# Two decoder layers on one core: pre-norm vectors multiplied onto the transposed activations, a fixed order for the first steps, and memory tokens turned by VectorE and DMA

## The chip, the cores and the metric

The kernel runs on one core of a Trainium2 chip. The metric is device microseconds from launch to end, the median of several runs. Five engines work side by side: TensorE (PE; its weight loads are listed apart as PEld), VectorE (DVE), ScalarE (ACT), GpSimd (POOL) and SyncE (SP). Each runs its own instructions in the order of its queue, and they meet at semaphores. In this kernel SP and POOL issue nearly all DMAs.

## The reference: what is computed

Two layers over 256 tokens of width 1024, all in float32. Each layer has three sub-layers, and each of these normalises its input with a vector of weights (the pre-norm), works, and normalises again before adding to the stream:

```python
def rms_norm(x, g):
    y = x * lax.rsqrt(jnp.mean(x * x, axis=-1, keepdims=True) + EPS)
    return y * g
def swiglu(h, w_in, w_out):
    a, b = jnp.split(h @ w_in, 2, axis=-1)
    return (jax.nn.silu(a) * b) @ w_out
for l in range(2):
    h = rms_norm(x, ffn1_norm_pre[l])
    x = x + 0.5 * rms_norm(swiglu(h, ffn1_w_in[l], ffn1_w_out[l]), ffn1_norm_post[l])
    h = rms_norm(x, mix_norm_pre[l])
    y = token_mixer(h, mem, ..., mem_norm[l], ...)   # conv, sparse attention, 256 memory tokens
    x = x + rms_norm(y, mix_norm_post[l])
    h = rms_norm(x, ffn2_norm_pre[l])
    x = x + 0.5 * rms_norm(swiglu(h, ffn2_w_in[l], ffn2_w_out[l]), ffn2_norm_post[l])
```

In the mixer the memory tokens are normalised with `mem_norm` and projected by `w_mem_kv` to keys and values. `w_in` of a feed-forward part is 1024 x 5632, `w_out` 2816 x 1024. Since a row's scale (the inverse root) factors out of a product, the kernel multiplies it on after the product; only the vector `g` has to meet the data or the weights before.

## The kernel before

**Products.** Every float32 operand is split into a high part (rounded to the format in which TensorE multiplies, fp32r) and a low part (the rest). A product of 128x128 by 128x512 is then three matmuls into one bank of PSUM: high by high, high activations by low weights, low activations by high weights (`mm3`, L337 to L340). Weights come from memory in units of 128x1024: SP loads `raw` (4 buffers), `split_unit` (L265) makes `whi` on ACT and `wlo` on DVE (8 buffers, four units). In units that follow a pre-norm the vector of that norm is multiplied on during this split, one value per row of weights, held in `gT` with one column per 128 rows (L280 and L281); where a unit holds two groups of 128 rows, each half of 512 columns is an instruction of its own. Other units are split plainly (L276 and L277).

**Activations.** `prenorm` (L442) turns x, 128 tokens by 1024, into 8 blocks of 128x128 with the tokens last: 8 transposes on PE into two banks (L381), then ACT rounds `hThi` out of PSUM (L372) and DVE subtracts `hTlo` (L373). The row scales (`rstd` L423, `rs` L450 to L453) run on ACT, DVE and POOL beside that. The mixer does the same with the merged branches before its output product.

**Turns.** The gated activations of a feed-forward part (`wide`, L501, made of two PSUM banks) go another way (`turn`, L388): DVE transposes blocks of 32x32 (`blocks`, L391), POOL writes them out in four DMAs (`there`, L396) and reads them back transposed in one (`moved`, L403); then ACT and DVE split them (`turnhi` L416, `turnlo` L417). A turn's parts are put into the program AWAY = 1, BACK = 3 and SPLIT = 8 steps after the transposition. The attention's probabilities take the same way.

**Memory.** `memory` (L605), one run per layer in the background, loads two tiles `m` of 128 memory tokens, calls `prenorm` on each (8 transposes on PE each), and then multiplies by `w_mem_kv`. `setup` (L534, called when the first output product of layer 1 has done 4 of 22 units) builds masks and loads small constants into `stage` by ten POOL DMAs (L587 to L591), which PE transposes (L593).

**Order.** Two streams, one per 128 tokens, are run as generators; a counter `now` of steps interleaves them, stream 0 ahead by up to LEAD = 3 steps. Both use the same weight unit, so a unit is 12 matmuls of 512 columns in the feed-forward input. Splits are put AHEAD = 4 steps before their use, loads 7. `later` defers a piece by some steps. A scheduler then orders every engine's instructions by its own model, except SP's queue, which stands in program order. PSUM has 6 banks for products and 2 for transposes.

**Start.** `keep_clock` (L164) runs 11 matmuls on a tile of zeros; the first vector is transposed on PE (L184) and copied to `gT` (L185); then x is transposed.

## Time and profile before

| what | value |
|---|---|
| median of 3 runs | 1281.77 us (1279.89 to 1281.87) |
| the profiled execution, its own time | 1282.43 us |
| its span, first to last instruction | 1280.5 us |
| mean granted TensorE clock | 0.996 of full speed |
| PE busy | 1259.4 us (98%) |
| DVE, ACT, POOL busy | 900.4, 770.7, 182.1 us |
| DMA | 280.58 MB, mean 219 GB/s |

The profile is of one execution. Its span begins with the first instruction and ends with the last; 1.93 us of its own time lie around that. The median of the runs is 0.66 us below the profiled execution. The busy times are read against the span: 98% of it on TensorE leaves 21.1 us in which it stood.

### The profile page before, as it was taken

The numbers are of one execution on the slowest core, as the hardware profiler recorded it, in microseconds if no ns is written. First come the engines' busy times: TensorE is split into PE (matmuls) and PEld (weight loads), VectorE is DVE, ScalarE is ACT, GpSimd is POOL, SyncE is SP. The second block draws the span as 40 slices with busy tenths as digits, with TensorE's granted clock in tenths as the row PEclk, the third lists the DMA queues.
The fourth block names the chain that finished last, engine by engine and source line by source line (L and its number), as shares of the span: only waits on it lengthen the run. The fifth ranks groups of instructions, "written<-read, shape, count | busy, mean of one in ns | idle before, by whom it ended". The sixth has DMA issues, their size and how long they took to land.

```text
span 1280.5 us, 16988 instructions
## 1 busy us (share of the span) xinstructions
PE 1259.4 (98%) x5898; PEld 1043.1 (81%) x5898; DVE 900.4 (70%) x1244; ACT 770.7 (60%) x1263; POOL 182.1 (14%) x384
## 2 busy tenths in 40 slices
PE   9999999999999999999999899999999999999996
PEld 7888788888888888888888788888888887888885
DVE  6767476879978676666566575668898876767752
ACT  6655366888875564554555455569887755555541
POOL 3101401302110011011001012013022100110110
PEclk9999999999999999999999999999999999999998
DMA  8777575776876657777767676757678756577770
GB/s 265 246 245 259 187 251 169 232 227 194 269 241 196 203 180 205 244 242 236 241 188 228 202 251 230 239 165 247 177 246 252 227 174 225 176 235 231 237 271 34
DMA packets 131877, 280.58 MB, mean 219 GB/s; under 512 B 11376, under 2 KB 30480, under 8 KB 131792
## 3 DMA queue, kind: packets, MB, share of 16 engines
q1 hardware_dynamic: 118256, 239.30, 59.6%
q0 software_dynamic: 13504, 40.20, 9.7%
q8 instruction: 46, 0.75, 0.2%
q14 instruction: 39, 0.32, 0.1%
q10 hardware_dynamic: 32, 0.01, 0.0%
HBM read 258.49 MB, written 20.97 MB: 218 GB/s over the span
## 4 chain that ended last, share of the span: by engine, by line
PE 89%; DMA 3%; ACT 2%; DVE 2%; issue 1%; POOL 1%; DVEq 0%; POOLq 0%; ACTq 0%
PE acc L338 19%; PE acc L340 19%; PE acc L339 19%; PE y L340 7%; PE y L339 6%; PE y L338 6%; PE pt L381 2%; DMA there<-blocks 2%; PE br L338 2%; PE br L340 2%; PE br L339 2%; PE o L856 1%; DMA moved<-there 1%; ACT whi L280 1%; PE s L834 1%
## 5 line engine op out<-in xcount | busy, mean ns | idle before, releaser
L280 ACT ACTIVATE whi<-raw,gT 128x512 fp32r<-128x512 f32 (+2 forms) x432 | 363.1, 873 | 232.2 <-PE acc L340 158.5
L281 DVE SCALAR_TENSOR_TENSOR wlo<-raw,gT,whi 128x512 fp32r<-128x512 f32 (+2 forms) x432 | 395.2, 936 | 153.1 <-ACT whi L280 151.2
L338 PE MATMUL acc<-whi,hThi 128*128 128x512 f32 (+1 forms) x1184 | 462.7, 391 | 4.1 <-DVE wide L501 3.2
L339 PE MATMUL acc<-wlo,hThi 128*128 128x512 f32 (+1 forms) x1184 | 459.6, 389 | 0.1
L340 PE MATMUL acc<-whi,hTlo 128*128 128x512 f32 (+1 forms) x1184 | 458.7, 388 | 0.0
L338 PEld LDWEIGHTS acc<-whi,hThi 128*128 128x128 f32 x1184 | 222.9, 188 | 48.1 <-DVE wide L501 3.6
L340 PEld LDWEIGHTS acc<-whi,hTlo 128*128 128x128 f32 x1184 | 222.7, 188 | 45.8 <-DVE hTlo L373 0.5
L339 PEld LDWEIGHTS acc<-wlo,hThi 128*128 128x128 f32 x1184 | 222.8, 188 | 43.4 <-DVE wlo L281 0.8
L277 DVE TENSOR_TENSOR wlo<-raw,whi 128x1024 fp32r<-128x1024 f32 x144 | 174.7, 1222 | 64.9 <-ACT whi L276 63.0
L276 ACT CAST whi<-raw 128x1024 fp32r<-128x1024 f32 x144 | 149.6, 1050 | 91.5 <-PE acc L340 50.9
L396 POOL DMA_DIRECT2D there<-blocks x160 | 87.9, 556 | 475.3 <-DVE blocks L391 472.0
L340 PE MATMUL y<-whi,turnlo 128*128 128x512 f32 x352 | 137.5, 391 | 0.0
L339 PE MATMUL y<-wlo,turnhi 128*128 128x512 f32 x352 | 137.4, 390 | 0.0
L338 PE MATMUL y<-whi,turnhi 128*128 128x512 f32 x352 | 136.4, 390 | 0.0
L417 DVE TENSOR_TENSOR turnlo<-moved,turnhi 128x1024 fp32r<-128x1024 f32 (+1 forms) x40 | 46.8, 1169 | 69.7 <-ACT turnhi L416 69.5
L416 ACT CAST turnhi<-moved 128x1024 fp32r<-128x1024 f32 (+1 forms) x40 | 40.3, 1008 | 79.4 <-DMA moved<-there 62.9
L339 PEld LDWEIGHTS y<-wlo,turnhi 128*128 128x128 f32 x352 | 66.1, 188 | 13.5
L340 PEld LDWEIGHTS y<-whi,turnlo 128*128 128x128 f32 x352 | 66.1, 188 | 13.5
L338 PEld LDWEIGHTS y<-whi,turnhi 128*128 128x128 f32 x352 | 66.0, 188 | 13.5
L431 POOL TENSOR_TENSOR nr<-nv,mhalf 128x1 f32<-128x1 f32 x28 | 19.0, 679 | 363.4 <-DVE nv L429 359.5
L403 POOL DMA_DIRECT2D moved<-there x40 | 22.4, 561 | 188.4 <-DMA there<-blocks 131.9
L496 ACT ACTIVATE th<-acc,rs 128x512 f32<-128x512 f32 (+1 forms) x48 | 30.9, 644 | 16.9 <-PE acc L340 16.9
(284 smaller groups left out, 1196.9 us busy)
## 6 DMA issues: line engine op xcount, KB each, us to landing
raw<-in_ffn_w_in_dram SPq DMA_DIRECT2D x160, 512.0 KB, 4.8
raw<-in_w_mix_in_dram SPq DMA_DIRECT2D x96, 512.0 KB, 4.7
raw<-in_ffn_w_out_dram SPq DMA_DIRECT2D x88, 512.0 KB, 5.0
there<-blocks POOLq DMA_DIRECT2D x128, 128.0 KB, 4.3
moved<-there POOLq DMA_DIRECT2D x32, 512.0 KB, 5.5
raw<-in_ffn_w_in_dram SPq DMA_DIRECT2D x32, 256.0 KB, 4.1
raw<-in_w_mem_kv_dram SPq DMA_DIRECT2D x16, 512.0 KB, 4.9
raw<-in_w_mix_out_dram SPq DMA_DIRECT2D x16, 512.0 KB, 4.3
```

The lines of the kernel that those rows point to most:

```text
L276: nc.scalar.copy(h, v)
L277: nc.vector.tensor_sub(w, v, f32(h))
L280: nc.scalar.activation(h, v, AF.Copy, scale=g)
L281: nc.vector.scalar_tensor_tensor(w, v, g, f32(h), op0=OP.mult, op1=OP.subtract)
L338: nc.tensor.matmul(ps, lhsT=xh, rhs=wh, start=start, stop=False, skip_group_check=skip)
L339: nc.tensor.matmul(ps, lhsT=xh, rhs=wl, start=False, stop=False, skip_group_check=skip)
L340: nc.tensor.matmul(ps, lhsT=xl, rhs=wh, start=False, stop=stop, skip_group_check=skip)
L381: nc.tensor.transpose(pt[:, j * P:(j + 1) * P], src[:, c0 + j * P:c0 + (j + 1) * P], ident)
L396: nc.gpsimd.dma_start(there[:, q * f:(q + 1) * f].rearrange("(p j) f -> j p f", j=32), blocks[q * 32:(q + 1) * 32, :n].rearrange("j (p f) ...
L416: nc.scalar.copy(hv, mv)
L417: nc.vector.tensor_sub(lv, mv, f32(hv))
L496: nc.scalar.activation(th[:, :n], pa[:, :n], AF.Tanh, scale=r_half)
```

## The change

1. The pre-norm vectors no longer go onto the weights. All units are split plainly, one instruction of 1024 columns per engine. `prenorm` multiplies the vector onto the transposed x: DVE writes `hf` from PSUM (two instructions of 128x512), ACT rounds `hThi` from `hf` in SBUF, DVE subtracts `hTlo`. In `product` the matmuls are ordered high by high for both banks, low activations for both, low weights for both.
2. In the first EARLY = 6 steps all instructions marked `pinned` keep program order. The start's 11 idle matmuls become 7 + 2 + 2 with the transposes between; splits are made 1 step ahead and the lead is 2 up to step RAMP = 10; the row scales come SCALES = 5 steps later; `ident_r` and the other norms' vectors wait for step 6, the transposition of `stage` comes STAGED = 8 steps after its loads, and `setup` is issued after the newest row sum.
3. BACK becomes 4 and SPLIT 12 for all turns. A memory tile is turned by `turn` instead of PE: `blocks`, `there`, `moved`, then DVE multiplies the vector on (`mf`), ACT rounds `mThi`, DVE subtracts `mTlo`.

The diff, cut to its core:

```diff
-AWAY, BACK, SPLIT = 1, 3, 8
+AWAY, BACK, SPLIT = 1, 4, 12
+EARLY, RAMP, SCALES, STAGED = 6, 10, 5, 8
...
+    def pinned(ins):
+        if first_steps[0] and not dry:
+            tc.keep_in_program_order(ins)
...
     def split_unit():
-        item, raw, segments = splits.pop(0)
+        item, raw, n = splits.pop(0)
...
-        for off, n, col in segments:
-            h, w, v = hi[:, off:off + n], lo[:, off:off + n], raw[:, off:off + n]
-            if col is None:
-                nc.scalar.copy(h, v)
-                nc.vector.tensor_sub(w, v, f32(h))
-            else:
-                g = gT[:, col:col + 1]
-                nc.scalar.activation(h, v, AF.Copy, scale=g)
-                nc.vector.scalar_tensor_tensor(w, v, g, f32(h), op0=OP.mult, op1=OP.subtract)
+        pinned(nc.scalar.copy(hi[:, :n], raw[:, :n]))
+        pinned(nc.vector.tensor_sub(lo[:, :n], raw[:, :n], f32(hi[:, :n])))
...
-        while splits and splits[0][0][0] <= now[0] + AHEAD and free["w"] > 0:
+        ahead = AHEAD if now[0] > RAMP else 1
+        while splits and splits[0][0][0] <= now[0] + ahead and free["w"] > 0:
...
-            for (_, n), p in zip(cols, ps):
-                mm3(p[:, :n], hT[0][:, k], hT[1][:, k], hi[:, off:off + n], lo[:, off:off + n], k == 0, k == 7)
-                off += n
+            for i, (x2, w) in enumerate(((0, hi), (1, hi), (0, lo))):
+                for j, p in enumerate(ps):
+                    n = cols[j][1]
+                    pinned(nc.tensor.matmul(p[:, :n], lhsT=hT[x2][:, k], rhs=w[:, j * n:(j + 1) * n],
+                                            start=(k == 0 and i == 0), stop=(k == 7 and i == 2)))
...
+    def prenorm(src, name, l, warm=False):
         hi, lo = gtile("hThi", F32R), gtile("hTlo", F32R)
+        g0 = PRE.index(name) * 16 + l * 8
+        hf = [ttile("hf") for _ in range(2)]
         for half in range(2):
-            transpose_split(src, None, hi, lo, half)
+            pt = transpose4(src, half * 512)
             if warm and WARM[1 + half]:
                 keep_clock(WARM[1 + half])
...
+            pinned(nc.vector.tensor_tensor(view(hf[half], 0, [[P, 4], [1, P]]), view(pt, 0, [[P, 4], [1, P]]),
+                                           view(gT, g0 + half * 4, [[1, 4], [0, P]]), op=OP.mult))
+        for half in range(2):
+            sl = slice(half * 512, (half + 1) * 512)
+            pinned(nc.scalar.copy(hi[:, sl], hf[half][:, :512]))
+            pinned(nc.vector.tensor_sub(lo[:, sl], hf[half][:, :512], f32(hi[:, sl])))
+            if warm and half == 0 and splits:
+                split_unit()
+        scale = norm_scales(src, SCALES if first_steps[0] else 0)
...
     def begin_layer(l):
         if l == 0:
-            setup()
+            with tc.issue_after(latest[0].ins):
+                setup()
...
-            H.append((yield from prenorm(m)))
-        yield 6
+            scale = norm_scales(m, 0)
+
+            def gained(mv, scale=scale):
+                hf, hi, lo = gtile("mf"), gtile("mThi", F32R), gtile("mTlo", F32R)
+                nc.vector.tensor_tensor(quarters(hf, 8), mv,
+                                        view(gT, PRE.index("mem_norm") * 16 + l * 8, [[1, 8], [0, 4], [0, 32]]),
+                                        op=OP.mult)
+                nc.scalar.copy(hi, hf)
+                nc.vector.tensor_sub(lo, hf, f32(hi))
+                H.append((tokens_last(hi, lo), scale))
+
+            turn(m, 1024, gained, SPLIT)
+            yield 3
+        yield SPLIT
...
-            t = 0 if steps[0] - steps[1] < LEAD else 1
+            t = 0 if steps[0] - steps[1] < lead and now[0] != START else 1
```

How the order of the instructions moves is shown at three places. The first is TensorE at the program's start; before, the names with `idle` are the matmuls on zeros, `x0` and `x1` the two token tiles, `whi` and `wlo` a weight unit.

```order
L164 MATMUL idle_90<-idle_88 128x512 x7
L164 MATMUL idle_143<-idle_88 128x512 x2
L164 MATMUL idle_153<-idle_88 128x512 x2
L184 MATMUL pt_112<-ident_102,first_98 128x16
L381 MATMUL pt_136<-ident_102,x0_86 128x128 x4
L381 MATMUL pt_146<-ident_102,x0_86 128x128 x4
L338 MATMUL acc_184<-whi_170,hThi_134 128x512
L338 MATMUL acc_185<-whi_170,hThi_134 128x512
L339 MATMUL acc_184<-wlo_171,hThi_134 128x512
L339 MATMUL acc_185<-wlo_171,hThi_134 128x512
L340 MATMUL acc_184<-whi_170,hTlo_135 128x512
L340 MATMUL acc_185<-whi_170,hTlo_135 128x512
```

```order
L171 MATMUL idle_90<-idle_88 128x512 x7
L196 MATMUL pt_111<-ident_102,first_98 128x16
L381 MATMUL pt_137<-ident_102,x0_86 128x128 x4
L171 MATMUL idle_142<-idle_88 128x512 x2
L381 MATMUL pt_146<-ident_102,x0_86 128x128 x4
L171 MATMUL idle_151<-idle_88 128x512 x2
L349 MATMUL acc_170<-whi_157,hThi_133 128x512
L349 MATMUL acc_171<-whi_157,hThi_133 128x512
L349 MATMUL acc_170<-whi_157,hTlo_134 128x512
L349 MATMUL acc_171<-whi_157,hTlo_134 128x512
L349 MATMUL acc_170<-wlo_158,hThi_133 128x512
L349 MATMUL acc_171<-wlo_158,hThi_133 128x512
```

Four idle matmuls moved behind the first transposes, and of the first unit the low weights now come last; x1 is transposed after 6 products, not 8.

The second place is VectorE around the memory tokens in layer 1, before: `hTlo` of `pt_1350` and `pt_1424` are the two memory tiles, `wlo` the weight splits beside them.

```order
L594 COPY smallT_122<-pt_1311 128x96
L277 TENSOR_TENSOR wlo_1403<-raw_1340,whi_1402 128x1024
L373 TENSOR_TENSOR hTlo_1349<-pt_1350,hThi_1348 128x512
L373 TENSOR_TENSOR hTlo_1349<-pt_1357,hThi_1348 128x512
L417 TENSOR_TENSOR turnlo_1391<-moved_1224,turnhi_1390 128x768
L429 SCALAR_TENSOR_TENSOR nv_1443<-ss2_1438 128x1
L373 TENSOR_TENSOR hTlo_1423<-pt_1424,hThi_1422 128x512
L373 TENSOR_TENSOR hTlo_1423<-pt_1431,hThi_1422 128x512
L277 TENSOR_TENSOR wlo_1453<-raw_1394,whi_1452 128x1024
L277 TENSOR_TENSOR wlo_1473<-raw_1412,whi_1472 128x1024
```

Now `blocks_1355` and `blocks_1445` (above this piece, behind `turnlo_1420`) are the turns of the two tiles, and this is what follows on the second:

```order
L417 TENSOR_TENSOR turnlo_1420<-moved_1313,turnhi_1419 128x768
L391 STREAM_TRANSPOSE blocks_1445<-m_1394 128x1024
L282 TENSOR_TENSOR wlo_1515<-raw_1482,whi_1514 128x1024
L282 TENSOR_TENSOR wlo_1535<-raw_1506,whi_1534 128x1024
L282 TENSOR_TENSOR wlo_1555<-raw_1524,whi_1554 128x1024
L282 TENSOR_TENSOR wlo_1559<-raw_1526,whi_1558 128x1024
L282 TENSOR_TENSOR wlo_1579<-raw_1538,whi_1578 128x1024
L643 TENSOR_TENSOR mf_1500<-moved_1396,gT_110 128x1024
L282 TENSOR_TENSOR wlo_1591<-raw_1546,whi_1590 128x1024
L647 TENSOR_TENSOR mTlo_1502<-mf_1500,mThi_1501 128x1024
L282 TENSOR_TENSOR wlo_1595<-raw_1562,whi_1594 128x1024
L643 TENSOR_TENSOR mf_1572<-moved_1480,gT_110 128x1024
```

The subtractions of `hTlo` out of PSUM are gone; a transposition of blocks per tile has come before, `mf` and `mTlo` after, with seven weight splits between the second tile's `blocks` and its `mf`.

The third place is VectorE in the first feed-forward part of layer 2, before: `blocks_6399` is the turn of stream 1's activations, `turnlo_6485` what comes of it, `wide_6521` the gate of stream 0's next columns.

```order
L391 STREAM_TRANSPOSE blocks_6399<-wide_6232 128x1024
L281 SCALAR_TENSOR_TENSOR wlo_6497<-raw_6466,gT_111,whi_6496 128x1024
L281 SCALAR_TENSOR_TENSOR wlo_6515<-raw_6488,gT_111,whi_6514 128x1024
L417 TENSOR_TENSOR turnlo_6433<-moved_6373,turnhi_6432 128x1024
L281 SCALAR_TENSOR_TENSOR wlo_6540<-raw_6506,gT_111,whi_6539 128x1024
L281 SCALAR_TENSOR_TENSOR wlo_6558<-raw_6531,gT_111,whi_6557 128x1024
L497 SCALAR_TENSOR_TENSOR th_6518<-th_6518,acc_6343 128x512
L281 SCALAR_TENSOR_TENSOR wlo_6583<-raw_6549,gT_111,whi_6582 128x1024
L281 SCALAR_TENSOR_TENSOR wlo_6601<-raw_6567,gT_111,whi_6600 128x1024
L417 TENSOR_TENSOR turnlo_6485<-moved_6436,turnhi_6484 128x1024
L501 SCALAR_TENSOR_TENSOR wide_6521<-th_6518,rs_5980,acc_6344 128x512
```

The same place in the changed kernel, where the turn of stream 1 is `blocks_6293`, stream 0's is `turnlo_6365`, and stream 0's next gate `wide_6411`:

```order
L391 STREAM_TRANSPOSE blocks_6293<-wide_6126 128x1024
L282 TENSOR_TENSOR wlo_6387<-raw_6356,whi_6386 128x1024
L282 TENSOR_TENSOR wlo_6405<-raw_6378,whi_6404 128x1024
L282 TENSOR_TENSOR wlo_6434<-raw_6396,whi_6433 128x1024
L282 TENSOR_TENSOR wlo_6452<-raw_6425,whi_6451 128x1024
L519 SCALAR_TENSOR_TENSOR th_6408<-th_6408,acc_6237 128x512
L417 TENSOR_TENSOR turnlo_6365<-moved_6275,turnhi_6364 128x1024
L523 SCALAR_TENSOR_TENSOR wide_6411<-th_6408,rs_5861,acc_6238 128x512
L282 TENSOR_TENSOR wlo_6477<-raw_6443,whi_6476 128x1024
L282 TENSOR_TENSOR wlo_6495<-raw_6461,whi_6494 128x1024
L417 TENSOR_TENSOR turnlo_6422<-moved_6336,turnhi_6421 128x1024
```

`turnlo_6422` and `turnlo_6485` both stand six weight splits behind the `blocks` of their turn; the gate that stood right behind it (`wide_6521`) now stands two splits ahead of it (`wide_6411`), and one more weight split and then the gate of stream 1 (`wide_6466`) follow.

On POOL's queue all ten loads of `stage` now stand ahead of the second `moved` of layer 1's last turn; five of the second block stood behind it.

## Rows read from the trace of the kernel before

**Rows 1.** The page: span, TensorE's busy time, and the shares of the chain of work that ended last.

```profile
span 1280.5 us, 16988 instructions
PE 1259.4 (98%) x5898; PEld 1043.1 (81%) x5898; DVE 900.4 (70%) x1244; ACT 770.7 (60%) x1263; POOL 182.1 (14%) x384
...
PE 89%; DMA 3%; ACT 2%; DVE 2%; issue 1%; POOL 1%; DVEq 0%; POOLq 0%; ACTq 0%
```

**Rows 2.** What TensorE waited for over the whole span: us in total, times, longest.

```profile
PE acc L338 <- DVE wide L501: 3.2, 1, 3.2
...
PE pt L593 <- DMA stage<-in_cmp_v_b_dram: 1.4, 1, 1.4
PE pt L381 <- DVE x L468: 1.2, 5, 0.3
PE acc L338 <- ACT hThi L372: 0.8, 1, 0.8
PE y L340 <- DVE mTlo L376: 0.4, 2, 0.2
```

**Rows 3.** TensorE's instructions around 710 us, in order of time: start, duration, line, names; in brackets idle time before and what ended it. Between the first two rows stand 11 more (12 starts from the one to the other), between the second and the last 9 that start at even steps from the third on (11 starts).

```profile
706.83 0.39 PE L340 MATMUL acc<-whi,hTlo 128*128 128x512 f32 x1
...
709.55 0.39 PE L340 MATMUL acc<-whi,hTlo 128*128 128x512 f32 x1
713.16 0.54 PE L338 MATMUL acc<-whi,hThi 128*128 128x512 f32 x1 [3.23 <-DVE wide L501]
...
713.93 0.63 PE L340 MATMUL acc<-whi,hTlo 128*128 128x512 f32 x1
...
716.49 0.58 PE L340 MATMUL acc<-whi,hTlo 128*128 128x512 f32 x1
716.91 0.40 PE L338 MATMUL acc<-whi,hThi 128*128 128x512 f32 x1
717.15 0.39 PE L339 MATMUL acc<-wlo,hThi 128*128 128x512 f32 x1
```

**Rows 4.** Stretches of the span: from:to, length, then busy time (and count) of PE, PEld, DVE, ACT, POOL, the granted clock, the DMA share, GB/s.

```profile
713.00:717.00 4.00, 3.84 (x10) 3.02 (x11) 3.78 (x5) 1.15 (x1) 0.00 (x0) 0.57 0.11 23
720.00:740.00 20.00, 20.00 (x90) 16.58 (x89) 13.91 (x14) 9.51 (x10) 2.18 (x4) 1.00 0.69 204
```

**Rows 5.** The turn in front of that wait, on DVE:

```profile
691.29 1.24 DVE L391 STREAM_TRANSPOSE blocks<-wide 128x1024 f32<-128x1024 f32 x1
...
711.23 1.22 DVE L417 TENSOR_TENSOR turnlo<-moved,turnhi 128x1024 fp32r<-128x1024 f32 x1 [3.54 <-ACT turnhi L416]
712.37 0.74 DVE L501 SCALAR_TENSOR_TENSOR wide<-th,rs,acc 128x512 f32<-128x512 f32 x1
```

**Rows 6.** The same on POOL and ACT:

```profile
695.59 2.20 POOL L396 DMA_DIRECT2D there<-blocks  x4 [2.97 <-issue]
703.29 0.56 POOL L403 DMA_DIRECT2D moved<-there  x1 [5.50 <-DMA there<-blocks]
...
710.15 1.04 ACT L416 CAST turnhi<-moved 128x1024 fp32r<-128x1024 f32 x1 [3.78 <-DMA moved<-there]
```

**Rows 7.** From the tables of two tiles, `there` and then `moved`: time from a DMA's issue to its landing.

```profile
DMA to landing us min/median/max: 2.3/4.7/7.8
DMA to landing us min/median/max: 3.3/5.4/7.8
```

**Rows 8.** The chain of work that ended last, between 140 and 165 us: start, duration, what.

```profile
145.57 0.57 POOL moved L403
...
148.13 3.08 DMA stage<-in_cmp_v_b_dram
...
158.16 0.87 PE pt L381 x8
```

**Rows 9.** Groups of instructions by line and shape: busy time and mean ns of one, idle time before and what ended it.

```profile
L281 DVE SCALAR_TENSOR_TENSOR wlo<-raw,gT,whi 128x1024 fp32r<-128x1024 f32 x160 | 204.7, 1283 | 108.4 <-ACT whi L280 107.8
L281 DVE SCALAR_TENSOR_TENSOR wlo<-raw,gT,whi 128x512 fp32r<-128x512 f32 x256 | 182.9, 745 | 43.8 <-ACT whi L280 42.5 <-ACT vf L951 0.3
L277 DVE TENSOR_TENSOR wlo<-raw,whi 128x1024 fp32r<-128x1024 f32 x144 | 174.7, 1222 | 64.9 <-ACT whi L276 63.0
L276 ACT CAST whi<-raw 128x1024 fp32r<-128x1024 f32 x144 | 149.6, 1050 | 91.5 <-PE acc L340 50.9 <-PE y L340 21.4 <-DMA raw<-in_ffn_w_out_dram 8.5
L373 DVE TENSOR_TENSOR hTlo<-pt,hThi 128x512 fp32r<-128x512 f32 x32 | 21.2, 687 | 10.0 <-ACT hThi L372 9.8
L372 ACT CAST hThi<-pt 128x512 fp32r<-128x512 f32 x32 | 17.6, 581 | 8.8 <-PE pt L381 8.6
L381 PE MATMUL pt<-ident,x 128*128 128x128 f32 x96 | 14.0, 275 | 1.2 <-DVE x L468 1.2
```

**Rows 10.** The start on PE and, in the last row, ACT's first weight split.

```profile
1.51 5.06 PE L164 MATMUL idle<-idle 128*128 128x512 f32 x11 [1.51 <-DVE idle L159]
...
6.72 1.17 PE L381 MATMUL pt<-ident,x 128*128 128x128 f32 x8
8.71 0.74 PE L338 MATMUL acc<-whi,hThi 128*128 128x512 f32 x2 [0.82 <-ACT hThi L372]
...
7.04 1.15 ACT L280 ACTIVATE whi<-raw,gT 128x1024 fp32r<-128x1024 f32 x1 [2.20 <-DVE gT L185]
```

**Rows 11.** From the stretch 0:20 of the same table of stretches as in rows 4 (70 on PE: 11 idle matmuls, 17 transposes, 42 products).

```profile
0.00:20.00 20.00, 17.56 (x70) 13.09 (x71) 10.60 (x15) 12.95 (x20) 10.08 (x43) 1.00 0.82 268
```

More of the change, by code (lines that the diff above doesn't have):

```diff
@@ L190, in other_gains, with turn @@
             nc.gpsimd.dma_start(rest[i * 16:(i + 1) * 16, 0:P], a[PRE[i + 1]].rearrange("l (k p) -> (l k) p", p=P))
-        pt = tbank()
-        nc.tensor.transpose(pt[:, :48], rest[0:48, 0:P], ident[0:48, 0:48])
-        nc.vector.tensor_copy(gT[:, 16:64], pt[:, :48])
+        def turn():
+            pt = tbank()
+            nc.tensor.transpose(pt[:, :48], rest[0:48, 0:P], ident[0:48, 0:48])
+            nc.vector.tensor_copy(gT[:, 16:64], pt[:, :48])
+        later(STAGED, turn)
     now = [0]
@@ L237, in load @@
         raw = rawp.tile([P, 1024], F32, name="raw")
-        segments = []
-        for off, step, name, l, k0, nk, c0, n, gains in parts:
+        width = 0
+        for off, step, name, l, k0, nk, c0, n in parts:
             dims = [[step, nk], [1, n]] if nk > 1 else [[1, n]]
@@ L591, in setup, with turn @@
             nc.gpsimd.dma_start(stage[b + 46:b + 48, 0:P], a["cmp_v_b1"][l].rearrange("(c p) -> c p", p=P))
-        pt = tbank()
-        nc.tensor.transpose(pt[:, :96], stage[0:96, 0:P], ident[0:96, 0:96])
-        nc.vector.tensor_copy(smallT, pt[:, :96])
+        def turn():
+            pt = tbank()
+            nc.tensor.transpose(pt[:, :96], stage[0:96, 0:P], ident[0:96, 0:96])
+            nc.vector.tensor_copy(smallT, pt[:, :96])
+        later(STAGED, turn)
     shared = {}
@@ L1224, in stream, with settled @@
             yield from ffn(t, l, 2)
+    def settled():
+        first_steps[0] = False
+        nc.vector.tensor_copy(ident_r, ident)
+        other_gains()
+    later(EARLY, settled)
     streams = [stream(0), stream(1)]
@@ L1233, in program @@
         able = [t for t in range(2) if live[t] and blocked[t] is None and resume[t] <= now[0]]
-        if not able or (able == [0] and live[1] and steps[0] - steps[1] >= LEAD):
+        lead = LEAD if now[0] > RAMP else 2
+        if not able or (able == [0] and live[1] and steps[0] - steps[1] >= lead):
             background()
```

95 lines of the change are left out of this document (46 added, 49 removed).

## The prediction

> **What bounds the kernel now.** The page comes first: TensorE is busy for 1259.4 us of a span of 1280.5 us and makes 89% of the chain of work that ended last [rows 1]. So a gain is work taken off TensorE, a wait of TensorE that goes, or a stretch at a low clock that goes. The next view is the list of what TensorE waited for: one wait of 3.2 us for a gate (`wide`, L501), one of 1.4 us for the `stage` loads, the rest under 1.3 us together each [rows 2]. The first looks small. The order in time shows its true size [rows 3]: in steady work 12 starts take 709.55 - 706.83 = 2.72 us, 0.227 us per matmul of 512 columns. From 709.55 to 717.15 there are 11 starts in 7.60 us where 11 x 0.227 = 2.5 us would do, so 5.1 us are lost. About 3.4 us of that is the wait, the rest a lower clock behind it: six starts from 713.93 to 716.49 take 0.427 us each, and the granted clock over 713 to 717 us is 0.57 against 1.00 later [rows 4]. [...]
>
> Why the gate was late: DVE transposed the blocks of stream 1 at 691.29 and was done by 692.53, POOL issued the write only at 695.59, `moved` was issued at 703.29 and its data reached ACT at 710.15, 17.6 us after the blocks. `turnlo` (711.23) stood in DVE's queue ahead of the other stream's gate (712.37), whose two banks TensorE needed [rows 5, 6]. A usual turn, from the landing times, is three more issues of a write (2.20 x 3/4 = 1.65), 4.7 to landing, 0.56 of issue and 5.4 to landing: 12.3 us, with ends at 7.8 and 17.8 [rows 6, 7].
>
> **The change, part by part.**
>
> *The stall at 710 us.* In the new order of DVE the gate stands two weight splits ahead of the other stream's `turnlo`. A split serves 12 matmuls, 12 x 0.227 = 2.72 us of TensorE. `turnlo_6422` stands six splits, 16.3 us, behind its blocks; stream 0's own, `turnlo_6365`, eight, 21.8 us. With a turn as slow as the one above, the first would be 17.6 + 1.04 - 16.3 = 2.3 us late, and behind it now waits a weight split, of which DVE is some two units (5.4 us) ahead, not the gate that TensorE waits for. I take the whole 5.1 us as a gain. Ends: 0, if some other piece comes late there, and 5.1.
>
> *Memory tiles.* 8 transposes of a tile take 0.87 us on TensorE's path [rows 8]; four tiles (two in each of two layers) go: -3.5 us. In exchange each tile costs DVE a transposition of blocks (1.24 [rows 5]) and a multiplication of 1024 columns. No row has the latter; between 1.22 (a subtraction of that size in SBUF) and 2 x 0.687 = 1.37 (two of 512 out of PSUM) [rows 9] I take 1.25. All this lies beside products, unless the turn is late. Of the second tile seven splits, 7 x 2.72 = 19.0 us, stand between its `blocks` and its `mf`. The turn needs 1.24 + 12.3 = 13.5 us, at most 19.0. Behind it come `mf` 1.25, `mThi` 1.05 and `mTlo` 1.22 before the products of that tile, on a DVE that also has splits of 1.22 between. Four later units are split there ahead of need, so a few microseconds of lateness are covered; I charge 0.3 us for each layer, with ends at 0 and 3.5 (the three steps exposed in full): +0.6 us. On POOL's queue each tile adds four `there` issues and a `moved` (some 2.8 us of issuing [rows 6], 4 tiles x 1 MB of traffic); POOL is 14% busy [rows 1], and behind them stand the small steps of the row scales and the next turns, none of them due before the memory products.
>
> *The loads of `stage`.* They were issued behind a `moved` that was itself waiting until 145.57, the last landed 3.08 us after 148.13 and TensorE waited 1.4 us [rows 2, 8]. Now all ten stand ahead of that `moved`, and the transposition comes 8 steps later: -1.4 us. Ends: 0 and 1.6.
>
> *Splits without the vectors.* DVE saves 160 x (1283 - 1222) ns = 9.8 us and, where two pieces of 512 become one of 1024, 128 x (2 x 745 - 1222) ns = 34 us; ACT gains likewise [rows 9]. TensorE waits for no split in its list [rows 2], so this is worth 0. The order of the three matmuls in `product` changes banks and loads, not their number: 0.
>
> *Pre-norms.* 24 multiplications of 0.69 us are added on DVE, each ahead of `hThi`: transposes, `hf` 0.69, `hThi` 0.58, `hTlo` 0.69 [rows 9], where `hf` was missing before. What hides it is the other stream's products. By the new order of TensorE, between a tile's transposes and the first product on its `hThi` there stand at least 7 matmuls (1.57 us) in the mixers' start and 10 to 19 (2.25 to 4.3 us) elsewhere. 0.69 + 0.58 = 1.27 us fits into all of them, `hTlo` (1.96) into most, and it is asked for later. I take 0, ends -1 and +2, since DVE may be in the middle of a split (1.22) when the transposes end.
>
> *The start.* Before, of the first 20 us TensorE used 42 x 0.227 + 16 x 0.109 = 11.3 us for products and transposes of x; 8.7 us are lost [rows 8, 11]. After: 11 idle matmuls took 5.06 us [rows 10], so 7 end at about 4.7; the vector, x0 and the other idle matmuls follow, and the first `hf` is done near 6.2. ACT then has `hThi` 0.58, `whi` 1.05 (its unit was there by 7.04 [rows 10]), `hThi`, `whi`; DVE's fixed queue ends `wlo` near 9.1, `hTlo` 9.8, `wlo` 11.0, two `hf` of x1 12.4, two `hTlo` 13.8 and the third `wlo` at 15.0. By then TensorE can have done 22 products and 16 transposes, 6.7 us, so 8.3 are lost, and 9.0 if each of 11 hand-overs costs some 0.06 us. Beyond that it runs steadily in both. +0.3 us, ends -0.4 and +1.3.
>
> The sum on the profiled execution: 1282.43 - 5.1 - 3.5 - 1.4 + 0.6 + 0.3 = 1273.3. The median lies 0.66 below the profiled execution: **1272.7 us**.
>
> **The rivals.**
>
> *A. The stall stays.* The wait for the gate, or another of that size, meets TensorE as before, since turns are as slow as they were and six splits are shorter than the slowest turn. For it: 16.3 against 17.6 + 1.04 us; and the write was issued 3 us late for no reason that the trace names ("issue" [rows 6]). It could also be an accident of the profiled execution, in which case there is nothing to gain. Against that: without it that execution would have been 1277.3, below all three runs (1279.89 to 1281.87). Time: 1272.7 + 5.1 = 1277.8.
>
> *B. The clock rises later.* Before, 11 plain matmuls in a row stood ahead of any transpose, and the products at 8.71 already ran fast. The idle matmuls' 0.46 us each is the low level's pace, though the granted clock of that stretch is given as 1.00 [rows 10, 11], so here the pace has to tell. Now only 7 stand in a row, with transposes among the rest. If the rise is put off by the first 12 products, each costs 0.427 - 0.227 = 0.20 more [rows 3]: 2.4 us, 1275.1.
>
> [...]
>
> *C. Slower: `hf` is not hidden.* At ten pre-norms behind the start (12 of x, less the two of the start; 96 transposes by 8 [rows 9]) both halves' multiplications, 2 x 0.69 us, are added in front of the first product, because DVE's queue holds splits at that moment. Price 10 x 1.38 = 13.8 us, 1286.5. It decides from 1.17 us each on (11.7 us in all, to come out 0.2% slower). For it: in the list of waits TensorE already waited 0.8 us once for `hThi`, and 1.2 us in five places for x [rows 2]. Against: the 7 to 19 matmuls in between; and few of the ten places are as short as 7.
>
> **How the numbers follow.** Forecast 0.60 (1270 to 1276.5, by the ends of mem, pre-norms and start). A 0.18, of which 0.14 is faster and 0.04 the same. B 0.10, faster. C 0.12, of which 0.09 is slower and 0.03, where only some of the places are exposed, the same. A measurement of this kernel tells about 0.2% (2.6 us) from no change: faster means under 1279.2, slower over 1284.3. Faster 0.84, same 0.07, slower 0.09. The range must hold the forecast, B and most of A: 1269 to 1279.5 leaves out C, a little of A and little below.
>
> **What would show it.** Right: no wait of TensorE over 1 us behind `wide` in layer 2's first feed-forward part, and no clock under 1.00 near it; TensorE's busy time about 3.5 us lower apart from the start; no wait for `stage`; DVE's busy time lower. Wrong: a wait for `mThi` or `mTlo` over 1 us in either layer; waits for `hThi` or `hTlo` at several of the ten pre-norms; matmuls at 0.43 us after 10 us. The forecast is most exposed where it takes 5.1 us from one wait: if that is there again at another gate, A's time comes out.

## The result, and the profile after

The changed kernel takes **1273.66 us** in the median (1271.39 to 1277.84, 7 runs) against 1281.77 for the kernel before (7 runs in the same session): ratio 0.9935, 95% interval 0.9911 to 0.9959. The forecast was 1272.7 in a range of 1269 to 1279.5. The total is right. Two terms of the sum are not, and they nearly cancel; and its largest term came true without needing the reason that the prediction gave. Ratios compare the fast executions of two kernels in one session, so they are not quite the quotients of the medians, and one execution of before (2570.11 us) and one of a_free_start (1394.73 us) were slow and enter none.

The profiled execution took 1271.95 us. Its page, span, busy engines and shares of the chain (against [rows 1]):

```profile
span 1270.2 us, 16756 instructions
PE 1255.8 (99%) x5866; PEld 1037.8 (82%) x5866; DVE 895.3 (70%) x1136; ACT 723.0 (57%) x1123; POOL 204.3 (16%) x404
...
PE 89%; ACT 4%; DVE 3%; DMA 2%; issue 2%; POOL 1%; DVEq 0%; POOLq 0%; ACTq 0%
```

32 instructions fewer on TensorE are the memory tiles' transposes. What TensorE waited for (against [rows 2]: us in total, times, longest):

```profile
PE pt L381 <- POOL kd L750: 2.0, 2, 1.0
...
PE pt L381 <- DVE x L490: 1.2, 5, 0.3
PE pt L787 <- DVE zs L942: 0.8, 2, 0.6
PE acc L349 <- ACT whi L281: 0.8, 1, 0.8
PE s L871 <- DVE gth L1244: 0.7, 1, 0.7
PE acc L337 <- ACT hThi L455: 0.4, 2, 0.2
PE y L339 <- DVE mTlo L376: 0.4, 2, 0.2
PE pt L381 <- ACT bs L1134: 0.4, 1, 0.4
```

The waits for `wide` and `stage` are gone. In their place stand small ones in the mixers: `zs`, `gth`, `hThi`, `bs`, more for `kd` (the one for `whi` is at the start, where before had one of the same size for `hThi`). None reaches 1.2 us, together they are about 2.9 us that the list of before does not have (`kd` 0.6 more, then 0.8, 0.7, 0.4 and 0.4).

The third view is the end of the program. TensorE's last matmul starts at 1269.24 in the trace of before and at 1263.89 now: 5.35 us earlier. The span is 10.3 us shorter. So almost half of what the profiled execution gained does not lie on TensorE at all. The instructions of the program's closing line show where; first before, then after (engine's queue, operation, count, duration in ns min/median/max, first and last start):

```profile
L1282 POOLq DRAIN  x3: 46/93/9170, 1270.6 to 1280.3; - x3
L1282 SPq DRAIN  x3: 7/7/7, 1274.8 to 1280.0; - x3
```

```profile
L1325 POOLq DRAIN  x3: 46/98/2312, 1265.2 to 1270.0; - x3
L1325 SPq DRAIN  x3: 7/7/7, 1269.4 to 1269.7; - x3
```

SP's first drain starts when the last output has landed (1274.8 before, where the last output was issued at 1272.6 and an output took 2.0 us to land). POOL's first drain (a closing instruction in its queue) began at 1270.6 and took 9.17 us, to 1279.8: 5.0 us in which nothing else ran. Now it takes 2.31 us and is over before the output has landed at 1269.4.

At the place of the old stall, VectorE, POOL and ACT after (against [rows 5, 6]):

```profile
708.40 1.23 DVE L417 TENSOR_TENSOR turnlo<-moved,turnhi 128x1024 fp32r<-128x1024 f32 x1 [2.27 <-ACT turnhi L416]
709.55 1.22 DVE L282 TENSOR_TENSOR wlo<-raw,whi 128x1024 fp32r<-128x1024 f32 x1
710.68 0.68 DVE L519 SCALAR_TENSOR_TENSOR th<-th,acc 128x512 f32<-128x512 f32 x1
711.40 0.75 DVE L523 SCALAR_TENSOR_TENSOR wide<-th,rs,acc 128x512 f32<-128x512 f32 x1
```

```profile
691.83 2.21 POOL L396 DMA_DIRECT2D there<-blocks  x4
700.52 0.56 POOL L403 DMA_DIRECT2D moved<-there  x1 [6.49 <-PE acc L349]
```

```profile
707.33 1.05 ACT L416 CAST turnhi<-moved 128x1024 fp32r<-128x1024 f32 x1 [2.44 <-DMA moved<-there]
```

The turn from the blocks' end (690.97) to `turnhi` took 16.4 us, VectorE stood 2.27 us for it, and TensorE did not notice: the gate ahead of it was done, the next one stands a weight split behind.

### The profile page after: what moved, and what is told of

The parts are those of the page before. It is cut to its first block, busy times and chain, and to the rows that moved or that the text cites. A ratio compares the mean times of both kernels' runs of the same rounds, so it can differ in the third digit from the quotient of the medians.

```text
span 1270.2 us, 16756 instructions
## 1 busy us (share of the span) xinstructions
PE 1255.8 (99%) x5866; PEld 1037.8 (82%) x5866; DVE 895.3 (70%) x1136; ACT 723.0 (57%) x1123; POOL 204.3 (16%) x404
## 4 chain that ended last, share of the span: by engine, by line
PE 89%; ACT 4%; DVE 3%; DMA 2%; issue 2%; POOL 1%; DVEq 0%; POOLq 0%; ACTq 0%
PE acc L349 34%; PE acc L339 8%; PE acc L337 8%; PE acc L338 8%; PE y L339 7%; PE y L338 7%; PE y L337 7%; PE pt L381 2%; PE br L337 2%; PE br L339 2%; PE br L338 2%; PE o L893 1%; ACT whi L281 1%; DVE wlo L282 1%; DMA raw<-in_cmp_v_w_dram 1%
## 5 line engine op out<-in xcount | busy, mean ns | idle before, releaser
L282 DVE TENSOR_TENSOR wlo<-raw,whi 128x1024 fp32r<-128x1024 f32 (+1 forms) x440 | 532.4, 1214 | 265.4 <-ACT whi L281 261.1
L281 ACT CAST whi<-raw 128x1024 fp32r<-128x1024 f32 (+1 forms) x440 | 458.3, 1046 | 380.2 <-PE acc L349 175.5
L349 PE MATMUL acc<-wlo,hThi 128*128 128x512 f32 x640 | 198.6, 390 | 0.1
L349 PE MATMUL acc<-whi,hThi 128*128 128x512 f32 x640 | 197.7, 390 | 0.8 <-ACT whi L281 0.8
L349 PE MATMUL acc<-whi,hTlo 128*128 128x512 f32 x640 | 197.2, 389 | 0.0
L337 PE MATMUL acc<-whi,hThi 128*128 128x512 f32 (+1 forms) x480 | 187.5, 391 | 0.4 <-ACT hThi L455 0.4
L338 PE MATMUL acc<-wlo,hThi 128*128 128x512 f32 (+1 forms) x480 | 184.9, 385 | 0.0
L339 PE MATMUL acc<-whi,hTlo 128*128 128x512 f32 (+1 forms) x480 | 184.7, 385 | 0.2
L349 PEld LDWEIGHTS acc<-whi,hThi 128*128 128x128 f32 x640 | 119.6, 188 | 26.1 <-ACT whi L281 1.2
L349 PEld LDWEIGHTS acc<-whi,hTlo 128*128 128x128 f32 x640 | 120.0, 188 | 25.4 <-DVE hTlo L456 0.4
L339 PEld LDWEIGHTS acc<-whi,hTlo 128*128 128x128 f32 x480 | 90.1, 188 | 18.4 <-DVE hTlo L456 0.6
L337 PEld LDWEIGHTS acc<-whi,hThi 128*128 128x128 f32 x480 | 90.3, 188 | 17.2 <-ACT hThi L455 1.3
```

The source lines that it names most:

```text
L281: pinned(nc.scalar.copy(hi[:, :n], raw[:, :n]))
L282: pinned(nc.vector.tensor_sub(lo[:, :n], raw[:, :n], f32(hi[:, :n])))
L337: nc.tensor.matmul(ps, lhsT=xh, rhs=wh, start=start, stop=False, skip_group_check=skip)
L338: nc.tensor.matmul(ps, lhsT=xh, rhs=wl, start=False, stop=False, skip_group_check=skip)
L339: nc.tensor.matmul(ps, lhsT=xl, rhs=wh, start=False, stop=stop, skip_group_check=skip)
L349: pinned(nc.tensor.matmul(p[:, :n], lhsT=hT[x2][:, k], rhs=w[:, j * n:(j + 1) * n], start=(k == 0 and i == 0), stop=(k == 7 and i == 2)))
```

## The experiments

All times are medians; "last matmul" is the start of TensorE's last matmul in the run's trace, "rest" is the span less that. They separate what TensorE gained from what the end gained. Names with a_ start from the changed kernel, those with b_ from the kernel before.

| kernel | median us | ratio to before (95%) | last matmul | rest | POOL's DMAs | its closing drain, us |
|---|---|---|---|---|---|---|
| before | 1281.77 | | 1269.24 | 11.3 | 218 | 9.17 |
| after | 1273.66 | 0.9935 (0.9911 to 0.9959) | 1263.89 | 6.3 | 238 | 2.31 |
| a_turns_old | 1273.68 | 0.9924 (0.9902 to 0.9946) | 1263.53 | 6.4 | 238 | 2.31 |
| b_turns_new | 1278.23 | 0.9962 (0.9945 to 0.9978) | 1263.82 | 11.3 | 218 | 9.17 |
| a_mem_pe | 1281.65 | 0.9981 (0.9963 to 0.9999) | 1269.04 | 11.3 | 218 | 9.17 |
| a_gain_weights | 1270.93 | 0.9903 (0.9879 to 0.9928) | 1259.72 | 6.4 | 238 | 2.31 |
| b_mem_turn | 1273.11 | 0.9933 (0.9913 to 0.9953) | 1264.50 | 6.4 | 238 | 2.31 |
| b_turns_mem | 1271.10 | 0.9917 (0.9898 to 0.9936) | 1262.34 | 7.5 | 238 | 2.31 |
| a_free_start | 1278.04 | 0.9967 (0.9946 to 0.9988) | 1269.43 | 6.4 | 238 | 2.31 |
| b_dma20 | 1280.11 | 0.9986 (0.9973 to 0.9999) | 1271.94 | 6.4 | 238 | 1.74 |
| b_dma20_late | 1272.81 | 0.9917 (0.9886 to 0.9948) | 1264.90 | 6.3 | 238 | 1.74 |
| b_dma10_late | 1283.22 (one run) | | 1269.92 | 11.6 | 228 | 9.42 |
| after_again | 1273.37 | 0.9910 (0.9882 to 0.9938) | 1265.31 | 6.4 | 238 | 2.31 |
| gain_weights_again | 1268.77 | 0.9870 (0.9845 to 0.9895) | 1261.06 | 6.3 | 238 | 2.31 |

The medians of before in the three later sessions were 1283.27, 1282.58 and 1287.05. The changed kernel itself ran in the first session and, as after_again, in the last; where a text below names its median without more, it is the first. Single executions of the kernel before range from 1277 to 1291 us, of the changed kernel from 1271 to 1278, of b_turns_new, but for one, from 1277 to 1280.

### The stall at the gate

The old step numbers in the changed kernel:

```diff
-AWAY, BACK, SPLIT = 1, 4, 12
+AWAY, BACK, SPLIT = 1, 3, 8
-            turn(m, 1024, gained, SPLIT)
+            turn(m, 1024, gained, 12)
-        yield SPLIT
+        yield 12
```

> The changed kernel with the old step numbers of a turn, BACK 3 and SPLIT 8 (the memory tiles keep 12). VectorE's order then has the gate (wide) right behind the other stream's turnlo again, in all feed-forward parts. Theory (the 5.1 us at 710 us came from that place in the order): at least one wait of TensorE for wide of 3 us or more with a clock under 1.00 behind it, and about 5 us more than the changed kernel, near 1278.5. Rival (the stall was an accident of one execution, or went with the lighter weight splits): no such wait, 1273.5 plus or minus 1.

The same time as the changed kernel, no wait for `wide`: the rival's forecast, not the theory's. VectorE's order did become the old one, the gate right behind `turnlo`:

```profile
706.39 1.22 DVE L417 TENSOR_TENSOR turnlo<-moved,turnhi 128x1024 fp32r<-128x1024 f32 x1
707.53 0.74 DVE L523 SCALAR_TENSOR_TENSOR wide<-th,rs,acc 128x512 f32<-128x512 f32 x1
```

`turnlo` has no idle time in front of it: this time the turn was quick, 12.3 us from blocks to landing (691.31 to 703.62). So the place in the order alone does not make the stall. The other way round, the new numbers in the kernel before:

```diff
-AWAY, BACK, SPLIT = 1, 3, 8
+AWAY, BACK, SPLIT = 1, 4, 12
```

> The kernel before with BACK 4 and SPLIT 12 and nothing else. Theory: the gate stands ahead of turnlo, TensorE's one wait for wide (3.2 us) and the low clock behind it are gone, about 5 us less than before, near 1276.7. Rival (accident, or the lighter splits did it): the same as before within 1 us, near 1281.8, or the wait comes again elsewhere.

5.0 us less than before in the median and no wait for `wide`: as the theory said. Both hold together if two things must meet: a slow turn and a gate behind it. The turn was as slow here as in before, 15.9 us from the blocks' end (691.03) to `turnhi`, and its write was issued as late, POOL standing 3.10 us for nothing that the trace names (2.97 in before [rows 6]):

```profile
694.10 2.20 POOL L396 DMA_DIRECT2D there<-blocks  x4 [3.10 <-issue]
```

```profile
706.91 1.05 ACT L416 CAST turnhi<-moved 128x1024 fp32r<-128x1024 f32 x1 [2.04 <-DMA moved<-there]
```

So the new place alone is enough. Two later kernels show the slow turn by itself, since their order on TensorE, VectorE and ScalarE is that of before, row by row (their idle loads on POOL lie 200 us earlier). The same two instructions of VectorE in b_dma10_late and in b_dma20_late:

```profile
713.39 1.23 DVE L417 TENSOR_TENSOR turnlo<-moved,turnhi 128x1024 fp32r<-128x1024 f32 x1 [1.02 <-ACT turnhi L416]
714.53 0.74 DVE L505 SCALAR_TENSOR_TENSOR wide<-th,rs,acc 128x512 f32<-128x512 f32 x1
```

```profile
708.29 1.22 DVE L417 TENSOR_TENSOR turnlo<-moved,turnhi 128x1024 fp32r<-128x1024 f32 x1
709.43 0.74 DVE L505 SCALAR_TENSOR_TENSOR wide<-th,rs,acc 128x512 f32<-128x512 f32 x1
```

One order, three executions: a turn of 17.6 us made TensorE wait 3.2 us [rows 2, 5, 6]; one of 15.1 us (b_dma10_late) made it wait 0.7 us; one of 12.5 us (b_dma20_late, to the landing) not at all. With the new place, 16.4 us (after) and 15.9 us (b_turns_new) cost nothing.

What makes the turn slow can be counted. The late write of before and of b_turns_new is the 122nd DMA that POOL issues. In all eleven traces without idle loads the 122nd DMA went out 2.65 to 3.07 us after both POOL and its blocks were ready; all other writes `there` went out within 0.31 us, but for a second stop that the next section shows. In the changed kernel the turns of layer 1's two memory tiles put ten DMAs in front, so the 122nd is another write, over 100 us earlier, behind which TensorE waits for nothing; it is the same in a_turns_old (586.59). With idle loads it is the 129th, in b_dma10_late within the turn ahead of the gate's and in b_dma20_late at 585.55. The rows of after, b_dma10_late and b_dma20_late:

```profile
586.25 2.19 POOL L396 DMA_DIRECT2D there<-blocks  x4 [3.19 <-issue]
```

```profile
693.17 1.09 POOL L396 DMA_DIRECT2D there<-blocks  x2 [2.64 <-issue]
```

```profile
585.55 1.09 POOL L396 DMA_DIRECT2D there<-blocks  x2 [2.74 <-issue]
```

So the stall went away in the changed kernel for either of two reasons: the gate's new place, or the held write's.

### The memory tiles and the end of the program

The changed kernel with the memory tiles on TensorE again:

```diff
-            scale = norm_scales(m, 0)
...
-            turn(m, 1024, gained, SPLIT)
-            yield 3
-        yield SPLIT
+            H.append((yield from prenorm(m, "mem_norm", l)))
+        yield 6
```

> The changed kernel with the memory tiles transposed on TensorE through prenorm again (hf multiplied on). Theory (32 transposes of 0.109 us on the bound engine): about 3.5 us more than the changed kernel, near 1277.2; TensorE's records show 32 more transposes. Rival (what the turns of m cost the mixers in waits eats the gain): within 1 us of the changed kernel, and the mixers' small waits of TensorE shrink by some 3 us.

8.0 us more instead of 3.5: neither theory nor rival had the end. The table splits it: the last matmul is 5.15 us later, the rest 5.0 us longer, because the drain is back at 9.17 us. On TensorE 3.5 us are transposes; another 2.4 us are one wait for `gth` in layer 1's mixer. The counterpart, in the kernel before, leaves the vectors on the weights:

```diff
-            H.append((yield from prenorm(m)))
-        yield 6
+            r = rstd([m[:, 0:512], m[:, 512:1024]])
...
+                nc.scalar.copy(hv, mv)
+                nc.vector.tensor_sub(lv, mv, f32(hv))
...
+            turn(m, 1024, halved, 12)
+            yield 3
+        yield 12
```

> The kernel before with the memory tiles turned by VectorE blocks and DMAs (vectors still on the weights, 12 steps for these turns alone). The runs so far showed that POOL's closing drain takes 9.2 us in every kernel that transposes the memory tiles on TensorE and 2.3 us in every one that turns them, which ends the span some 5 us earlier. Theory (the turns carry both): TensorE ends about 3.3 us earlier, the drain falls to 2.3 us, together about 8 us less than before, near 1275. Rival (the drain's length hangs on something else in the change, such as the lighter splits): the drain stays at 9.2 us and the time falls by 3.3 at most, near 1280.

9.5 us less than before, the drain 2.31 us. The last matmul is 4.7 us earlier, more than the transposes' 3.5: the held write is at 587.71, and the waits for `wide` come to 1.2 us (two of 0.7 at most) in place of the stall. This part alone gives as much as the whole change.

What in the turns shortens the drain? POOL issues 20 more DMAs. Added to the kernel before without any use:

```diff
+        if t == 0 and l == 0 and which == 2:
+            spare = ttile("spare")
+            for i in range(20):
+                nc.gpsimd.dma_start(spare[2 * i:2 * i + 2, 0:P], a["cmp_k_b1"][0].rearrange("(c p) -> c p", p=P))
```

> The kernel before plus 20 loads of two rows of 128 values each by POOL at the start of layer 1's second feed-forward part, into a tile that nobody reads, so that POOL issues 238 DMAs as in the changed kernel instead of 218. Theory (the drain at the end hangs on how many DMAs POOL has issued): the drain falls from 9.2 to 2.3 us and the time by about 5 us, near 1278. Rival (it hangs on the bytes or the kind of the turns): the drain stays at 9.2 us and the time the same as before.

The drain fell to 1.74 us and the rest to 6.4. The time fell by 2.5 only, because at that place the loads stood ahead of a row scale of x on POOL: TensorE waited 3.3 us for x, and the mean granted clock of the profiled execution was 0.996, against 0.999 in b_dma20_late. With `t == 1` in the condition they come behind it:

> The 20 idle POOL loads once more, added to the kernel before, but behind the pre-norms of layer 1's second feed-forward part, where no row scale of x waits behind them (at the earlier place they held x up by 3.3 us). Theory (the number of POOL's DMAs sets the closing drain, and nothing else is touched): drain near 2 us, TensorE's end as in the kernel before, 5 us less, near 1277.5. Rival: the drain at 9.2 us, 1282.5.

1272.81 us, the time of the changed kernel, from 20 loads that nobody reads. 5.0 us of it are the rest; the last matmul is 4.3 us earlier too, which the theory did not expect: it is the quick turn shown above, since the loads also moved the held write away from it. With 10 loads:

> The same with 10 idle loads, 228 DMAs by POOL. If the drain falls evenly with their number, it takes 5 to 6 us; if it is a step or a count that starts over, it takes about 9 or about 2 us.

The closing instructions of b_dma10_late, then of b_dma20_late:

```profile
L1286 POOLq DRAIN  x3: 46/93/9417, 1271.3 to 1281.2; - x3
```

```profile
L1286 POOLq DRAIN  x3: 46/93/1740, 1266.2 to 1271.0; - x3
```

It does not fall evenly: 9.17 us with 218 DMAs, 9.42 with 228, 1.74 or 2.31 with 238. It fits a count that starts over, and the held DMAs show where. A second one followed 104 DMAs behind the first: the 226th in every kernel with 238 DMAs and no idle loads, the 233rd in the two with 20 idle loads. Kernels with 218 or 228 DMAs end before it. In after:

```profile
1180.58 1.10 POOL L396 DMA_DIRECT2D there<-blocks  x2
1184.00 1.10 POOL L396 DMA_DIRECT2D there<-blocks  x2 [2.32 <-issue]
```

From the last held DMA to the end POOL issues 96 more in before (218 - 122), 99 in b_dma10_late, 12 in after, 5 in b_dma20_late, and the drains are 9.17, 9.42, 2.31 and 1.74 us: all four are 1.33 us and 0.0817 us for each of these DMAs. Twenty unused loads of two rows of 512 bytes shorten it (1.74 us) as well as the turns' megabytes (2.31 us); with both POOL gets past the second held DMA. POOL does not wait there for a transfer: in before its last DMA was issued at 1227.36, 43 us ahead of the drain, and a turn's transfer landed after 7.8 us at most [rows 7]. Why POOL stops at these counts stays open, and why the idle loads move the count by seven, ten loads like twenty.

The last matmul of b_dma10_late is late (1269.92) for a cause of its own: TensorE waited 4.4 us at 143 us for the loads of the other norms' vectors (`rest`), a wait of 0.8 us at most in the others.

### The vectors on the activations

The changed kernel with the pre-norm vectors on the weights again, `hf` gone:

```diff
-        pinned(nc.scalar.copy(hi[:, :n], raw[:, :n]))
-        pinned(nc.vector.tensor_sub(lo[:, :n], raw[:, :n], f32(hi[:, :n])))
+        for off, n, col in pieces(item[3], n):
...
+                pinned(nc.scalar.activation(h, v, AF.Copy, scale=g))
+                pinned(nc.vector.scalar_tensor_tensor(w, v, g, f32(h), op0=OP.mult, op1=OP.subtract))
...
-            pinned(nc.vector.tensor_tensor(view(hf[half], 0, [[P, 4], [1, P]]), view(pt, 0, [[P, 4], [1, P]]),
-                                           view(gT, g0 + half * 4, [[1, 4], [0, P]]), op=OP.mult))
+            hf.append(pt)
```

> The changed kernel with the vectors of the three pre-norms on the weights again and no hf (the memory tiles keep mf). In the trace of the changed kernel TensorE lost about 4 us more in the mixers than before. Theory (hf, one more VectorE step ahead of hThi, and the splits' new lengths are the cause): the loss goes, near 1269.7, and no wait for hThi at the mixers' start. Rival (the mixers' loss comes from the longer SPLIT and the later memory work): within 1 us of the changed kernel, 1273.7. Against both: splits in two pieces of 512 take ACT and VectorE longer; if that binds somewhere the time rises.

2.7 us less than the changed kernel's median of the first session; the last matmul 4.17 us earlier. What TensorE waits for in it:

```profile
PE pt L408 <- POOL kd L775: 1.4, 2, 0.7
PE pt L408 <- DVE x L515: 1.2, 5, 0.2
PE br L364 <- ACT gth L1255: 0.4, 1, 0.4
PE y L366 <- DVE mTlo L403: 0.2, 1, 0.2
```

`zs`, `bs` and `hThi` are gone from the list, `kd` and `gth` are shorter. Both kernels once more, on one chip:

> The changed kernel as it is, on the same chip as the next one, to compare the two directly: 1273.7.

> The changed kernel with the vectors of the three pre-norms back on the weights, as before (a_gain_weights). Theory (hf is a net loss of some 3 us): 2 to 4 us under the changed kernel on the same chip, 1270 to 1271.5. Rival (the first difference was that of two chips or of chance): within 1 us of it.

1273.37 and 1268.77: 4.6 us apart, the last matmul 1265.31 and 1261.06, 4.25 apart. No execution of one reaches the range of the other (1270.77 to 1278.19, and 1267.27 to 1269.13). So the first part of the change costs some 4 us, `hf` and the plain splits taken together, and a version without them beats both kernels: 0.9870 (0.9845 to 0.9895) of the time before. The new order of the matmuls in `product` stays in both; no run tests it.

### The fixed start

```diff
-        if first_steps[0] and not dry:
+        if False:
-        ahead = AHEAD if now[0] > RAMP else 1
+        ahead = AHEAD
-        lead = LEAD if now[0] > RAMP else 2
+        lead = LEAD
-            t = 0 if steps[0] - steps[1] < lead and now[0] != START else 1
+            t = 0 if steps[0] - steps[1] < lead else 1
```

> The changed kernel with no instruction pinned in the first steps, splits 4 steps ahead and a lead of 3 from the start. Theory (the fixed start repairs what hf would cost there): the first 20 us of TensorE lose more than the 8.9 us of the changed kernel, by 0.5 to 2 us, and the time is 1274 to 1276. Rival (it brings nothing): within 0.5 us of the changed kernel, 1273.7. The start of the kernel before, without hf, lost 8.7 us.

4.4 us more than the changed kernel in the first session, beyond the expectation; the last matmul is 5.5 us later. The start in stretches (length, busy time and count of PE, PEld, DVE, ACT, POOL, granted clock, DMA share, GB/s):

```profile
0.00:20.00 20.00, 13.71 (x44) 10.28 (x45) 10.90 (x15) 9.81 (x12) 6.21 (x35) 0.74 0.80 257
8.00:10.00 2.00, 1.03 (x4) 0.71 (x4) 0.91 (x2) 0.41 (x1) 0.00 (x0) 0.60 0.92 270
10.00:12.00 2.00, 0.08 (x1) 0.00 (x0) 1.34 (x2) 0.63 (x1) 0.00 (x0) 0.50 1.05 400
12.00:16.00 4.00, 3.46 (x12) 2.68 (x13) 3.77 (x6) 3.76 (x5) 0.00 (x0) 0.50 0.77 246
```

TensorE's 44 instructions stand against 69 in the changed kernel (below): 25 x 0.227 = 5.7 us. Without fixed order weight splits come ahead of `gT` and `hf` on VectorE, TensorE waits 2.3 us for the one and 2.5 us for the other, and its granted clock was 1.00 over 6 to 8 us, 0.60 over 8 to 10 us and 0.50 over 10 to 16 us. The first wait ended at 8.97: the four transposes ahead of it took 0.66 us, the four behind it 1.11 us. The changed kernel's start:

```profile
0.00:20.00 20.00, 17.64 (x69) 12.74 (x70) 14.07 (x25) 12.22 (x20) 10.07 (x43) 1.00 0.74 243
```

### All but the vectors and the fixed start

b_turns_mem is the kernel before with BACK 4 and SPLIT 12, the turn of the memory tiles as in b_mem_turn, and this:

```diff
-        pt = tbank()
-        nc.tensor.transpose(pt[:, :96], stage[0:96, 0:P], ident[0:96, 0:96])
-        nc.vector.tensor_copy(smallT, pt[:, :96])
+        def turn_stage():
+            pt = tbank()
+            nc.tensor.transpose(pt[:, :96], stage[0:96, 0:P], ident[0:96, 0:96])
+            nc.vector.tensor_copy(smallT, pt[:, :96])
+
+        later(8, turn_stage)
```

> The kernel before with BACK 4 and SPLIT 12, the memory tiles turned, and the transposition of stage 8 steps later: all of the change but the multiplication on the transposed tiles and the fixed start. Theory (these three carry all the gain, hf costs some 3 us): 5 + 8 us less than before, near 1270, not slower than the changed kernel with the vectors back on the weights (1270.9). Rival (the fixed start or the lighter splits carry a part): 1273 or more.

1271.10 us, 1.1 more than expected. It is 2.0 us less than b_mem_turn, and the intervals overlap: the 5 and the 8 us do not add up. That fits the count: once the memory tiles are turned, the held write no longer stands ahead of the gate, and the new step numbers have little left to repair.

## Why the prediction was right, and where it was not

**The stall (-5.1): right in size, and in part by luck.** The wait is gone. The prediction gave one reason, the gate's new place in VectorE's order, and b_turns_new shows that this place is enough: 5.0 us less, with the write held as before. But the changed kernel did not need it: a_turns_old, with the old place, is as quick, because the memory tiles' ten DMAs moved the held write to 586 us. Of this the prediction had nothing. Rival A's point, a write issued 3 us late for no reason that the trace names, was the open end; it is no accident of one execution but POOL's 122nd DMA, late in all eleven traces without idle loads (with them the 129th, in all three). Why single executions of before spread over 13 us, and those of the changed kernel over 7, is not shown.

**The memory tiles (-3.5 on TensorE, +0.6 in waits): right on TensorE.** 32 transposes are gone, and no wait for `mThi` or `mTlo` of the memory reaches 0.5 us. What their 20 DMAs do to POOL's count, to the stall and to the end, had no term.

**The loads of `stage` (-1.4): right.** The wait is gone from the list.

**Splits without vectors (0): right as far as shown.** VectorE and ScalarE became lighter (895.3 and 723.0 us against 900.4 and 770.7), and a_gain_weights, with the heavier splits, is faster. No run changes the splits alone.

**The pre-norms (0, ends -1 and +2): wrong.** This is the step that failed: "0.69 + 0.58 = 1.27 us fits into all of them". The cover was counted as matmuls on TensorE; what VectorE and ScalarE had in their queues at that moment was left to the ends of the range, and the price lies beyond these: a_gain_weights and its repetition put `hf`, less what the plain splits give back, at 4.2 us of TensorE's time in both pairs. Of it 0.7 to 1.4 us lie in the start (69 TensorE instructions against 75 in the first 20 us, 68 against 71 in the repetition, 0.227 us each), the rest in the mixers: in the two pairs the same matmuls fall 2.1 and 2.8 us further behind between 215 and 320 us, in layer 1's, and 0.9 and 1.8 us between 840 and 1050 us, in layer 2's. Only 0.4 us is a wait for `hThi` itself: most comes out later, at `zs` and `gth` (VectorE), `bs` (ScalarE) and `kd` (POOL). That the delay is handed on to these through the queues is argued, not shown. So `hf` is not hidden, as rival C said, but at a third of its price and mostly at other places than in front of the first product.

**The start (+0.3): right, its steps within 0.7 us.** Forecast were the first `hf` done near 6.2, two `hf` of x1 at 12.4, the third `wlo` at 15.0; VectorE shows:

```profile
6.17 0.69 DVE L451 TENSOR_TENSOR hf<-pt,gT 128x512 f32<-128x512 f32 x1 [0.87 <-PE pt L381]
...
11.40 1.28 DVE L451 TENSOR_TENSOR hf<-pt,gT 128x512 f32<-128x512 f32 x2
...
14.32 1.23 DVE L282 TENSOR_TENSOR wlo<-raw,whi 128x1024 fp32r<-128x1024 f32 x1 [0.26 <-ACT whi L281]
```

They end at 6.86, 12.68 and 15.55, and TensorE has begun 41 products by 20 us instead of 42. For a hand-over the forecast had some 0.06 us, the author's estimate; from the end of the first `hf` (6.86) to `hThi` (6.89) it took 0.03 us. Rival B did not come. The granted clock does not settle it, since it is given as 1.00 over the start of before too, where the idle matmuls took 0.46 us each [rows 10, 11], about as long as the 0.427 us from start to start in a stretch with a granted clock of 0.57 [rows 3, 4]; TensorE's own pace does:

```profile
5.01 1.11 PE L381 MATMUL pt<-ident,x 128*128 128x128 f32 x4
5.78 1.07 PE L171 MATMUL idle<-idle 128*128 128x512 f32 x2
6.68 0.60 PE L381 MATMUL pt<-ident,x 128*128 128x128 f32 x4
7.04 0.71 PE L171 MATMUL idle<-idle 128*128 128x512 f32 x2
8.51 0.73 PE L349 MATMUL acc<-whi,hThi 128*128 128x512 f32 x2 [0.76 <-ACT whi L281]
```

Four transposes take 1.11 us and then 0.60, two matmuls 1.07 and then 0.71: the pace rose in between, with transposes among the idle matmuls, and the first products take 0.73 us for two, as in before (0.74 [rows 10]). The start of a_free_start has a lower granted clock: 0.60 over 8 to 10 us, where the first of two waits of over 2 us ended at 8.97.

**The end of the program (no term): missing.** The prediction summed up TensorE and took what lies behind its last matmul as given. That stretch was 11.3 us and is 6.3 us; the row of the closing drain was there to be read in the trace of before. That the change shortens it is luck: its 20 DMAs carry POOL past the second held DMA, and from there 12 DMAs are left to the end instead of 96 (drains of 2.31 and 9.17 us). With it and with `hf` at its price, the sum on the profiled execution would be -9.1 - 5.0 + 4.2 = -9.9; measured were 1271.95 - 1282.43 = -10.5.

So the total was hit by luck: a gain of 5.0 us that was not seen and a cost of 4.2 us that was taken as hidden cancel.

## What to carry to other kernels

A step that is added between a transposition and its first product must be checked against the queues of the engines that run it, not only against the matmuls beside it: here 0.69 us of "hidden" work at each of twelve pre-norms cost 4 us together, most of it at waits with other names. Read the program's last microseconds too: here a closing instruction of POOL ran on for 5.0 us after the last output had landed. And a wait of an engine that the trace puts down to nothing ("issue") is worth counting: in all 14 traces POOL stopped at the same few numbers of its DMAs (122 and 226, with idle loads 129 and 233). Twenty loads that nobody reads moved these stops, and the time of before fell to 0.9917 of itself with the order of TensorE, VectorE and ScalarE untouched.
